# A two-layer decoder trunk in split fp32r: seven raw weight buffers for four, eight Strassen blocks for seven, and the next layer's transposes one block forward

## The chip, the core and the metric

The kernel runs on one core of one Trainium2 chip. The time is that of one execution on the device, in microseconds; lower is better. Three runs of the kernel before are shown, and their median stands for it. Beside them one execution was profiled: its trace gives for every instruction the engine, the start, the duration and what it waited for. Engines are written as the profile writes them: PE is TensorE's matmul, PEld its weight load, DVE is VectorE, ACT is ScalarE, SP is SyncE, whose queue issues the loads.

## The reference

Two layers are applied to 256 tokens of 1024 features, in fp32. Each layer has a mixing part (three branches from one wide input projection, merged by gates) and an MLP with a squared ReLU; each part is normalised before and after and added to h.

```python
# per layer; T = 256, D_MODEL = 1024, D_FF = 4096
u = rms_norm(h, norm_mix_pre)
z = u @ w_in                      # q | k | v | rnn_x | rnn_y | pool | gates
mix = gated_merge(z, attention(q, k, v) @ w_attn_br,
                  gelu(rnn_y) * rg_lru(conv4(rnn_x)) @ w_rnn_br,
                  multi_scale_pool(pool) @ w_pool_br) @ w_out
h = h + rms_norm(mix, norm_mix_post)
m = rms_norm(h, norm_mlp_pre)
hid = relu(m @ w_mlp_up) ** 2     # 256 x 4096
h = h + rms_norm(hid @ w_mlp_down, norm_mlp_post)
```

## The kernel before

**Products in three passes.** Every fp32 operand is split into a part hi in the type fp32r and a remainder lo (`split`: ACT copies the source into hi, L90; DVE subtracts it from the source, L91). A product is the sum of hi x hi, hi x lo and lo x hi, three matmuls into one PSUM bank (`mm3`, L98 to L100; `by_pass`, L309, does the same in three sweeps).

**Weights.** All weights of both layers are packed as 316 units of 128 x 1024 fp32, 512 KB each, in the order of use. `load_to` takes a buffer of the pool `raws` and issues the load on SP's queue (L140). `split_to(n)` splits units up to n into the pools `his` and `los` (eight buffers each: names wh and wl), and then calls `load_to(n + 3)`, so that the loads run three units ahead with the four raw buffers. A raw buffer is free again when both ACT's copy and DVE's subtraction have read it; SP's queue works in order, and a load whose buffer isn't free holds up what stands behind it. PSUM has eight banks, handed out in turn from one pool; tmp has 28 buffers of 2 KB per partition, acts three of each kind.

**The MLP.** The hidden width is cut into 16 blocks of 256. An up unit (`up`, through `w_unit`) makes one block's hidden values for all tokens: 48 matmuls of 256 columns, then Relu (L735) and Square on ACT, which leave z. The down product of a block is a 256 x 256 by 256 x 1024 matrix product. For the first `nstr = NBLK - PLAIN` blocks it is done by Strassen's seven products in Winograd's form (`down`): seven products of 128 x 128 by 128 x 512, accumulated over the blocks in seven PSUM banks (pr), 21 matmuls of 512 columns a block in place of 24. They need sums: `weight_sums` adds halves of two raw units on DVE (wsum, L763, L767, L768) and splits the first (dh, dl) and a half of the second (bh, bl); `weight_forms` splits the two sums (sh, sl, one name for both); `hidden_forms` makes four differences of the hidden values on DVE (sm, L746 to L749) and splits them and z itself into xf, in two pieces of 384 and 512 columns. `drain` combines the seven banks. The remaining `PLAIN` blocks are plain (`hidden_split`, `plain`: 24 matmuls); the last `LAST = 3` of them run together, one quarter of the output after the other (tokens tt, columns nh).

**How the two are interleaved.** `UPS` says how many up units stand in each Strassen block: one up unit, four products, another up unit, three products; or, with one, the up unit and then all seven products. The first up unit of a block is also the place at which the sums and hidden forms of the next block are issued. While the Strassen part runs, seven PSUM banks hold products and the eighth (ps) takes the up units in turn, so that an up unit's first matmul waits for the Relu of the one before it. `up_first` makes the first two blocks' hidden values another way: in rows by tokens, with wh as the moving operand (ps <- mh), followed by transposes. In it, `mlp_in(1)` makes the second half of the MLP's input: transposes of h on PE (L222, `to_features`), copies to mh on ACT (L228), remainders ml on DVE (L230).

**The seam between layers.** After the first 128 tokens' last plain block, `residual(0)` (square sums on ACT, yg on DVE L270, h L275) and `mix_norm(0)` (un, L321) run while the other 128 tokens' plain blocks go on; `mix_features(0)` then transposes un (L222) and makes uh (ACT L228) and ul (DVE L230), and `residual(1)`, `mix_norm(1)` follow at the end. The next layer's first matmuls (ps <- wh,uh, L309) read uh and ul.

**What sets the order.** The program is written in the order above, but a scheduler orders the instructions of each engine by priority: the place in the program, and 200 places earlier for what is wrapped in `hp` (residual, mix_norm, mix_features and the MLP's to_features). An instruction on one engine's list waits for its operands in its turn, with all behind it. Which buffers and which waits arise follows from these lists and from the pools' sizes. GpSimd does nearly nothing; all transfers are issued by SP, but for two small ones by ACT.

Of the kernel before, what the change touches and what calls it, by code (L numbers as in the profile page):

```python
# [16 lines left out]
L = 2  # L17
# [6 lines left out]
HU_COLS = 1024  # L24
HP = 200
WARM = 12
NRAW = 4
NTMP = 28
NHI = 8
MID = 1  # L30
# [3 lines left out]
RGD = 4  # L34
FINE = (8, 8)

PLAIN = 9
LAST = 3

UPS = (2, 2, 2, 2, 2, 2, 1)  # L40
NBLK = 16
SQRT_2_PI = 0.7978845608028654

# [15 lines left out]
def trunk(ctx, tc, x, wts, rgw, par, gpost, eye, ctab, out):  # L59
    nc = tc.nc  # L60
    V, A, PE, G = nc.vector, nc.scalar, nc.tensor, nc.gpsimd

    const = ctx.enter_context(tc.tile_pool(name="const", bufs=1))
    raws = ctx.enter_context(tc.tile_pool(name="raws", bufs=NRAW))
    his = ctx.enter_context(tc.tile_pool(name="his", bufs=NHI))
# [13 lines left out]
    def ttile(shape, dt=F32, nm="t"):  # L79
        return tmp.tile(shape, dt, tag="t", name=nm)  # L80
# [7 lines left out]
    def split(hi, lo, src, scale=None):  # L88
        if scale is None:
            A.activation(hi, src, AF.Copy)  # L90
            V.tensor_tensor(out=lo, in0=src, in1=hi.bitcast(F32), op=ALU.subtract)  # L91
        else:
            A.activation(hi, src, AF.Copy, scale=scale)
            V.scalar_tensor_tensor(out=lo, in0=src, scalar=scale, in1=hi.bitcast(F32),
                                   op0=ALU.mult, op1=ALU.subtract)
# [34 lines left out]
    st = {"load": 0, "split": 0, "use": 0}  # L130
# [5 lines left out]
    def load_to(n):  # L136
        while st["load"] < min(n, NHU):
            i = st["load"]
            r = raws.tile([P, HU_COLS], F32, tag="raw", name=f"raw{i}")
            nc.sync.dma_start(r[:], wts[i])  # L140
            raw_t[i] = r
            st["load"] += 1

    def split_to(n):
        while st["split"] < min(n, NHU):
            i = st["split"]
            load_to(i + 1)
            r = raw_t.pop(i)
            wh = his.tile([P, HU_COLS], F32R, tag="wh", name=f"wh{i}")
            wl = los.tile([P, HU_COLS], F32R, tag="wl", name=f"wl{i}")  # L150
            parts = 2 if i in fine else 1
            for k in range(parts):
                sl = slice(k * HU_COLS // parts, (k + 1) * HU_COLS // parts)
                split(wh[:, sl], wl[:, sl], r[:, sl])
            hu_t[i] = (wh, wl)
            st["split"] += 1
        load_to(n + 3)

    def take(n):
        split_to(st["use"] + n)  # L160
        r = [hu_t.pop(st["use"] + i) for i in range(n)]
        st["use"] += n
        return r

    def ahead():
        split_to(st["use"] + AHEAD)
# [91 lines left out]
    @hp  # L258
    def residual(tt, banks, scale, gB):

        yg = []
        ss = stile(2)
        for nh in range(2):
            square_sum(banks[nh][:], ss[:, nh:nh + 1], scale)
            t = ttile([P, 512], nm="yg")
            gs = gB[:, nh * 512:(nh + 1) * 512]
            if isinstance(scale, float):
                V.tensor_tensor(out=t[:], in0=banks[nh][:], in1=gs, op=ALU.mult)
            else:
                V.scalar_tensor_tensor(out=t[:], in0=banks[nh][:], scalar=scale, in1=gs, op0=ALU.mult, op1=ALU.mult)  # L270
            yg.append(t)
        rs = rsqrt(total(ss))
        for nh in range(2):
            sl = slice(nh * 512, (nh + 1) * 512)
            V.scalar_tensor_tensor(out=h[:, tt, sl], in0=yg[nh][:], scalar=rs, in1=h[:, tt, sl],  # L275
                                   op0=ALU.mult, op1=ALU.add)
# [38 lines left out]
    @hp  # L315
    def mix_norm(tt):
        rstd = rsqrt(sumsq(halves(tt)))
        u = []
        for x_ in halves(tt):
            t = ttile([P, 512], nm="un")  # L320
            V.tensor_scalar(t[:], x_, rstd, None, op0=ALU.mult)  # L321
            u.append(t)
        return u

    @hp
    def mix_features(tt, u, l):
        to_features(tt, u, prm[:, l, PG_PRE:PG_PRE + 8], uh, ul)
# [3 lines left out]
    nc.sync.dma_start(h[:, 1, :], x[P:T, :])  # L331
    un = [mix_norm(0)]
    split_to(1)
    to_features(0, un[0], prm[:, 0, PG_PRE:PG_PRE + 8], uh, ul, between=lambda: split_to(2))
    split_to(3)
# [4 lines left out]
    for l in range(L):  # L340
# [357 lines left out]
        nc.sync.dma_start(gB[:], gpost[l, 1])  # L698
        nstr = NBLK - PLAIN
        prods = {}  # L700
# [30 lines left out]
        def up(j):  # L731
            ps = w_unit(take(2), uh, ul)
            tick()
            z = ttile([P, 2, T], nm="z")
            A.activation(z[:], ps[:], AF.Relu)  # L735
            A.activation(z[:], z[:], AF.Square)
            zs[j] = z
# [18 lines left out]
        def weight_sums(j):  # L756

            load_to(st["split"] + 2)
            r0, r1 = raw_t.pop(st["split"]), raw_t.pop(st["split"] + 1)
            st["split"] += 2  # L760
            st["use"] += 2
            t8 = acts.tile([P, 4, 512], F32, tag="lo", name="wsum")
            V.tensor_tensor(out=t8[:, 0:2, :], in0=r0.rearrange("p (b n) -> p b n", b=2),  # L763
                            in1=r1[:, 0:512].unsqueeze(1).to_broadcast([P, 2, 512]), op=ALU.add)
            w1 = (his.tile([P, HU_COLS], F32R, tag="wh", name="dh"), los.tile([P, HU_COLS], F32R, tag="wl", name="dl"))
            w4 = (ttile([P, 512], F32R, nm="bh"), ttile([P, 512], F32R, nm="bl"))
            V.tensor_tensor(out=t8[:, 2, :], in0=t8[:, 0, :], in1=r0[:, 512:1024], op=ALU.add)  # L767
            V.tensor_tensor(out=t8[:, 3, :], in0=t8[:, 2, :], in1=r1[:, 512:1024], op=ALU.add)  # L768
            split(w1[0][:], w1[1][:], r0[:])
            split(w4[0][:], w4[1][:], r1[:, 512:1024])  # L770
            wforms[j] = [w1, w4, t8]
            load_to(st["split"] + 3)

        def weight_forms(j):
            t8 = wforms[j].pop()
# [5 lines left out]
        def down(j, part):  # L781
            f = forms[j]
            w1, w4, w2, w3 = wforms[j]
            lo_, up_ = slice(0, 512), slice(512, 1024)

            for p, blk, w, cs in ((1, 2, w1, up_), (3, 6, w1, lo_), (2, 0, w4, lo_), (7, 5, w2, lo_), (5, 3, w2, up_),
                                  (6, 4, w3, lo_), (4, 1, w3, up_))[part]:
                if p not in prods:
                    prods[p] = bank([P, 512], nm="pr")
                first, last = j == 0, j == nstr - 1 and p in (1, 5, 6, 7)  # L790
                mm3(prods[p][:], f[:, 0, blk, :], f[:, 1, blk, :], w[0][:, cs], w[1][:, cs], first, last)
# [9 lines left out]
        for j in range(nstr):  # L801
            for i in range(UPS[j]):
                up(nup)
# [4 lines left out]
                if nup < NBLK:  # L808
                    split_to(st["use"] + 2)
                down(j, slice(0, 7) if UPS[j] == 1 else (slice(0, 4), slice(4, 7))[i])  # L810
            del forms[j], wforms[j]
# [20 lines left out]
        def plain(j, hus, tt, nh):  # L832
            for k in range(2):
                wh, wl = hus[k]
                cs, tsl = slice(nh * 512, (nh + 1) * 512), slice(tt * P, (tt + 1) * P)
                mm3(tgt[tt][nh][:], hids[j][:, 0, k, tsl], hids[j][:, 1, k, tsl], wh[:, cs], wl[:, cs],
                    tt == 1 and nh == 1 and j == nstr and k == 0, j == NBLK - 1 and k == 1)
# [22 lines left out]
        for tt in range(2):  # L860
            for nh in range(2):
                for b in range(LAST):
                    if tt == 1 and nh == 1 and b == LAST - 1 and l + 1 < L:
                        mix_features(0, un[0], l + 1)
                    plain(NBLK - LAST + b, hus[2 * b:2 * b + 2], tt, nh)
            ys = [rest[tt][nh] for nh in range(2)]
            for nh in range(2):
                V.tensor_tensor(out=ys[nh][:], in0=tgt[tt][nh][:], in1=ys[nh][:], op=ALU.add)
            residual(tt, ys, msq[tt], gB)
            if l + 1 < L:  # L870
                un.append(mix_norm(tt))
            else:
                for hf in range(2):
                    sl = slice(hf * 512, (hf + 1) * 512)
                    nc.sync.dma_start(out[tt * P:(tt + 1) * P, sl], h[:, tt, sl])
# [37 lines left out]
def _layout(i):  # L913
    qc = np.concatenate([np.arange(hd * 64, hd * 64 + 64) for hd in _HEADS])
    units, rg, par, gp = [], [], [], []
    for l in range(L):
# [18 lines left out]
        dn = i["w_mlp_down"][l].reshape(NBLK, 2, P, D)  # L935
        nstr = NBLK - PLAIN
        pairs = [np.stack([np.concatenate([d[c][:, 512:], d[1 - c][:, :512]], 1) for c in range(2)]) for d in dn]
        units += [up[0], up[1], up[2], pairs[0], up[3]]
        nup = 3
        for j in range(nstr):  # L940
            for n in range(UPS[j]):
                nup += 1
# [28 lines left out]

# [10 lines left out]
```

## Time and profile before

| | |
|---|---|
| median of 3 runs | 961.85 us (959.25 to 962.14) |
| the profiled execution's own time | 960.85 us |
| its span in the trace | 959.1 us |
| granted TensorE clock | 0.996 |
| DMA, mean over the span | 181 GB/s, 173.29 MB in all |
| L91 on DVE (subtractions for lo) | x316, 349.8 us, mean 1126 ns |
| L90 on ACT (copies to hi) | x316, 302.2 us, mean 987 ns |
| loads of raw units, median from issue to landing | 4.3 us |

How to read the rows that follow: a group of instructions reads line, engine, operation, output <- inputs, partitions x elements; a row that begins with a time gives the start within the span and the duration in us, and in brackets the wait just before it and what ended it. A matmul's duration reaches into the next one's, so that a TensorE row's duration isn't what it costs; the distance of the starts is. In a row of a stretch of time, the figures behind its bounds are length, then busy time (and instructions) of PE, PEld, DVE, ACT, POOL and SP, the granted clock, the busy share of the 16 DMA engines and their GB/s. A row of the waits gives the wait's sum, its count and its longest.

### The profile page before, as it was taken

Reading aid. Unit: us, or ns where it says so; the run is one execution under the profiler, and the core shown is the slowest. Engines: PE = TensorE matmul, PEld = TensorE weight load, DVE = VectorE, ACT = ScalarE, POOL = GpSimd, SP = SyncE. Lnnn points to the kernel's source line nnn. Section 1 sums busy time; section 2 is a strip of 40 time slices with the busy share of each in tenths; the row PEclk is TensorE's granted clock in tenths of the full one; section 3 lists DMA queues with packets and bytes.
Section 4 is the critical chain, followed back from the end, with each engine's and each line's share of the span. In section 5 each row is a group of like instructions: output and inputs, shape, how many; then the busy total and the mean of one; then the engine's idle time right before and its main releaser. Section 6 shows DMA issues by size and latency. Waiting matters only on the chain.

```text
span 959.1 us, 15057 instructions
## 1 busy us (share of the span) xinstructions
PE 946.3 (99%) x5674; PEld 827.5 (86%) x5674; DVE 730.0 (76%) x1253; ACT 620.5 (65%) x1049; POOL 2.6 (0%) x20
## 2 busy tenths in 40 slices
PE   8999999999999999999999999999999999999997
PEld 5898988988888998998878989788888899999885
DVE  6878786779768987867586769777897599787753
ACT  7754864788736766675376657556895467666741
POOL 0000000000000000000000000000000000000000
PEclk9999999999999999999999999999999999999999
DMA  7766456453754556566457536536358265646641
GB/s 269 250 201 194 132 158 205 149 192 111 243 174 154 208 170 209 168 216 217 132 178 255 171 123 194 186 114 221 123 174 262 90 210 186 223 169 207 197 151 44
DMA packets 48745, 173.29 MB, mean 181 GB/s; under 512 B 5408, under 2 KB 5792, under 8 KB 48672
## 3 DMA queue, kind: packets, MB, share of 16 engines
q1 hardware_dynamic: 48384, 172.16, 54.7%
q8 instruction: 44, 0.72, 0.3%
q14 instruction: 29, 0.24, 0.1%
q10 hardware_dynamic: 288, 0.17, 0.1%
HBM read 171.26 MB, written 1.05 MB: 180 GB/s over the span
## 4 chain that ended last, share of the span: by engine, by line
PE 88%; DMA 5%; DVE 4%; ACT 1%; issue 1%; DVEq 0%; SPq 0%; ACTq 0%
PE ps L98 20%; PE ps L100 20%; PE ps L99 20%; PE ps L309 7%; DMA raw<-wts 5%; PE pr L100 5%; PE pr L99 5%; PE pr L98 5%; PE ps L397 1%; PE ps L445 1%; DVE wl L91 1%; PE ps L434 1%; ACT wh L90 1%; PE ps L222 0%; PE ps L377 0%
## 5 line engine op out<-in xcount | busy, mean ns | idle before, releaser
L91 DVE TENSOR_TENSOR wl<-raw,wh 128x1024 fp32r<-128x1024 f32 (+1 forms) x316 | 349.8, 1126 | 121.4 <-ACT wh L90 113.8
L90 ACT ACTIVATE wh<-raw 128x1024 fp32r<-128x1024 f32 (+1 forms) x316 | 302.2, 987 | 192.7 <-PE ps L100 60.2
L98 PE MATMUL ps<-mh,wh 128*128 128x256 f32 x448 | 127.2, 284 | 1.3 <-ACT z L735 1.3
L100 PE MATMUL ps<-mh,wl 128*128 128x256 f32 x448 | 126.8, 283 | 0.0
L99 PE MATMUL ps<-ml,wh 128*128 128x256 f32 x448 | 126.7, 283 | 0.0
L98 PE MATMUL ps<-uh,wh 128*128 128x256 f32 x384 | 109.0, 284 | 0.0
L99 PE MATMUL ps<-ul,wh 128*128 128x256 f32 x384 | 108.6, 283 | 0.0
L100 PE MATMUL ps<-uh,wl 128*128 128x256 f32 x384 | 108.6, 283 | 0.0
L98 PEld LDWEIGHTS ps<-mh,wh 128*128 128x128 f32 x448 | 85.9, 192 | 3.7 <-ACT z L735 2.8
L99 PEld LDWEIGHTS ps<-ml,wh 128*128 128x128 f32 x448 | 85.9, 192 | 0.7
L100 PEld LDWEIGHTS ps<-mh,wl 128*128 128x128 f32 x448 | 85.9, 192 | 0.0
L98 PE MATMUL ps<-wh,uh 128*128 128x512 f32 x200 | 79.8, 399 | 1.0 <-ACT uh L228 1.0
L100 PE MATMUL ps<-wh,ul 128*128 128x512 f32 x200 | 78.6, 393 | 0.1
L99 PE MATMUL ps<-wl,uh 128*128 128x512 f32 x200 | 78.5, 393 | 0.0
L98 PEld LDWEIGHTS ps<-uh,wh 128*128 128x128 f32 x384 | 73.6, 192 | 1.1 <-issue 0.7
L99 PEld LDWEIGHTS ps<-ul,wh 128*128 128x128 f32 x384 | 73.6, 192 | 0.4
L100 PEld LDWEIGHTS ps<-uh,wl 128*128 128x128 f32 x384 | 73.6, 192 | 0.0
L98 PE MATMUL pr<-wh,hid 128*128 128x512 f32 x144 | 56.1, 390 | 0.0
L100 PE MATMUL pr<-wh,hid 128*128 128x512 f32 x144 | 56.0, 389 | 0.0
L99 PE MATMUL pr<-wl,hid 128*128 128x512 f32 x144 | 56.0, 389 | 0.0
L98 PEld LDWEIGHTS ps<-wh,uh 128*128 128x128 f32 x200 | 37.9, 189 | 11.1 <-issue 2.3
L100 PEld LDWEIGHTS ps<-wh,ul 128*128 128x128 f32 x200 | 37.9, 189 | 8.9 <-DVE ul L230 0.8
(234 smaller groups left out, 1916.5 us busy)
## 6 DMA issues: line engine op xcount, KB each, us to landing
raw<-wts SPq DMA_DIRECT2D x316, 512.0 KB, 4.3
gB<-gpost SPq DMA_DIRECT2D x4, 512.0 KB, 5.4
rg<-rgw SPq DMA_DIRECT2D x8, 256.0 KB, 3.8
out<-h SPq DMA_DIRECT2D x4, 256.0 KB, 2.0
h<-x SPq DMA_DIRECT2D x2, 256.0 KB, 3.6
h<-x SPq DMA_DIRECT2D x1, 512.0 KB, 7.5
cst<-ctab SPq DMA_DIRECT2D x1, 168.0 KB, 3.7
prm<-par ACTq DMA_DIRECT2D x1, 104.0 KB, 4.0
```

The lines of the kernel that those rows point to most:

```text
L90: A.activation(hi, src, AF.Copy)
L91: V.tensor_tensor(out=lo, in0=src, in1=hi.bitcast(F32), op=ALU.subtract)
L98: PE.matmul(o, lh, rh, start=start, stop=False, **kw)
L99: PE.matmul(o, lh, rl, start=False, stop=False, **kw)
L100: PE.matmul(o, ll, rh, start=False, stop=stop, **kw)
L309: PE.matmul(o, xx[:, c, tsl], ww[c], start=(n == 0 and c == 0), stop=(n == 2 and c == 7))
L397: PE.matmul(sc[hd // hp][:, hd % hp, :], qT[a, j // 2][rows, j % 2, blk * P:(blk + 1) * P], kTs[0][rows, a, 0:w], start=True, stop=True)
L434: PE.transpose(ps[:, g, :], g8["p"](4 * b + g)[:, kt * P:(kt + 1) * P], ident)
L445: PE.matmul(ps[b * 64:b * 64 + 64, :, :], vt[kt][:, 256 + kv * 64:256 + kv * 64 + 64], g8[b, kt][:], start=(kt == 0), stop=(kt == nk - 1))
```

## The change

The edit has four parts.

- The pool `raws` has seven buffers instead of four, and the two calls that load ahead reach six units ahead instead of three (in `weight_sums`, five units past the pair just taken instead of three). The kernel is built with a smaller area in SBUF for DMA descriptors (`dynamic_dma_scratch_size=1024` bytes per partition, where the default was 16384).
- `PLAIN` is 8 instead of 9: eight blocks of 16 go by Strassen's seven products.
- `UPS` spreads the 13 up units over eight Strassen blocks as 2, 2, 2, 1, 2, 1, 2, 1 instead of 2, 2, 2, 2, 2, 2, 1 over seven. `_layout` packs the units in that order.
- `mix_features(0)` of the next layer is called ahead of the last plain block but one of the last quarter, instead of ahead of the last.

```diff
-NRAW = 4
+NRAW = 7
...
-PLAIN = 9
+PLAIN = 8
 LAST = 3

-UPS = (2, 2, 2, 2, 2, 2, 1)
+UPS = (2, 2, 2, 1, 2, 1, 2, 1)
...
             st["split"] += 1
-        load_to(n + 3)
+        load_to(n + NRAW - 1)
...
             wforms[j] = [w1, w4, t8]
-            load_to(st["split"] + 3)
+            load_to(st["split"] + NRAW - 2)
...
                 for b in range(LAST):
-                    if tt == 1 and nh == 1 and b == LAST - 1 and l + 1 < L:
+                    if tt == 1 and nh == 1 and b == LAST - 2 and l + 1 < L:
                         mix_features(0, un[0], l + 1)
...
-    nc = bacc.Bacc("TRN2", target_bir_lowering=False, num_devices=1)
+    nc = bacc.Bacc("TRN2", target_bir_lowering=False, num_devices=1, dynamic_dma_scratch_size=1024)
```

What it moves is seen in each engine's list. On SP three more raw loads of the first layer stand ahead of the constants table (cst, L337), and the first gain row (gB, L668) stands at place 28 of the list instead of 11; the number of loads is the same. On PE there are 5668 matmuls instead of 5674: 48 fewer of pr <- hid (432 to 384) and 42 more of pr <- xf (294 to 336).

**The MLP's start, on PE.** The place is `up_first` of the first layer: by_pass over the first 128 tokens, with the transposes of h (operand idt, the identity) for the other 128 put in. Before:

```order
L309 MATMUL ps<-wh_3201,mh 128x256 x4
L309 MATMUL ps<-wh_3207,mh 128x256 x4
L309 MATMUL ps<-wh_3201,ml 128x256 x3
L222 MATMUL ps<-idt,h 128x128 x4
L309 MATMUL ps<-wh_3201,ml 128x256
L222 MATMUL ps<-idt,h 128x128 x4
L309 MATMUL ps<-wh_3207,ml 128x256 x4
L309 MATMUL ps<-wl_3202,mh 128x256 x4
```

And after the change, where the numbers of the names are others but 3207, 3213 and 3208 stand for the same weights as 3201, 3207 and 3202 above:

```order
L309 MATMUL ps<-wh_3207,mh 128x256 x4
L309 MATMUL ps<-wh_3213,mh 128x256 x4
L309 MATMUL ps<-wh_3207,ml 128x256 x4
L309 MATMUL ps<-wh_3213,ml 128x256 x4
L222 MATMUL ps<-idt,h 128x128 x4
L309 MATMUL ps<-wl_3208,mh 128x256
L222 MATMUL ps<-idt,h 128x128 x4
L309 MATMUL ps<-wl_3208,mh 128x256 x3
```

Five more matmuls stand ahead of the transposes of h.

**The same place, on DVE.** h is finished at L275; then come the first weight sum (L763), the remainders ml of the second 128 tokens (L230) and the square of the first hidden values (zt, L726). Before:

```order
L275 SCALAR_TENSOR_TENSOR h<-yg,s,h 128x512 x2
L91 TENSOR_TENSOR wl_3356<-raw_3213,wh_3355 128x512
L763 TENSOR_TENSOR wsum<-raw_3215,raw_3361 128x1024
L230 SCALAR_TENSOR_TENSOR ml<-ps,prm,mh 128x128 x8
L726 TENSOR_TENSOR zt<-zt 128x512
L767 TENSOR_TENSOR wsum<-wsum,raw_3215 128x512
L91 TENSOR_TENSOR dl<-raw_3215,dh 128x1024
```

And after:

```order
L275 SCALAR_TENSOR_TENSOR h<-yg,s,h 128x512 x2
L763 TENSOR_TENSOR wsum<-raw_3201,raw_3203 128x1024
L91 TENSOR_TENSOR dl<-raw_3201,dh 128x1024
L230 SCALAR_TENSOR_TENSOR ml<-ps,prm,mh 128x128 x8
L726 TENSOR_TENSOR zt<-zt 128x512
L767 TENSOR_TENSOR wsum<-wsum,raw_3201 128x512
L91 TENSOR_TENSOR wl_3452<-raw_3219,wh_3451 128x1024
```

The remainder dl of the first block's weights stands ahead of the eight ml pieces instead of behind them, and one half of a wl that stood behind h has gone ahead of it.

**A Strassen block, on DVE.** The place is the fourth block of the first layer, which has two up units before and one after. Ahead of the rows shown, both lists have the next block's first sum (wsum, L763), dl, a wl, the first piece of xf and a second wl. Before:

```order
L91 TENSOR_TENSOR wl126_4208<-raw126_4119,wh126_4207 128x1024
L91 TENSOR_TENSOR wl127_4212<-raw127_4139,wh127_4211 128x1024
L91 TENSOR_TENSOR bl_4110<-raw123_4032,bh_4109 128x512
L746 TENSOR_TENSOR sm_4121<-z_3642 128x128
L747 TENSOR_TENSOR sm_4121<-z_3642 128x128
L748 TENSOR_TENSOR sm_4121<-sm_4121,z_3642 128x128
L749 TENSOR_TENSOR sm_4121<-z_3642,sm_4121 128x128
L91 TENSOR_TENSOR sl_4229<-wsum_4105,sh_4228 128x1024
L91 TENSOR_TENSOR xf_4126<-sm_4121,xf_4126 128x512
L763 TENSOR_TENSOR wsum_4288<-raw128_4141,raw129_4215 128x1024
```

And after, in the block with one up unit:

```order
L767 TENSOR_TENSOR wsum_4230<-wsum_4230,raw126_4038 128x512
L768 TENSOR_TENSOR wsum_4230<-wsum_4230,raw127_4040 128x512
L91 TENSOR_TENSOR sl_4171<-wsum_4111,sh_4170 128x1024
L91 TENSOR_TENSOR sl_4175<-wsum_4111,sh_4174 128x1024
L91 TENSOR_TENSOR bl_4116<-raw123_3960,bh_4115 128x512
L746 TENSOR_TENSOR sm_4125<-z_3648 128x128
L747 TENSOR_TENSOR sm_4125<-z_3648 128x128
L748 TENSOR_TENSOR sm_4125<-sm_4125,z_3648 128x128
L749 TENSOR_TENSOR sm_4125<-z_3648,sm_4125 128x128
L91 TENSOR_TENSOR dl_4233<-raw126_4038,dh_4232 128x1024
L91 TENSOR_TENSOR wl128_4255<-raw128_4123,wh128_4254 128x1024
L91 TENSOR_TENSOR xf_4130<-sm_4125,xf_4130 128x512
```

The two wl of the second up unit (126 and 127) are gone, since those units are now the block's weights; both sl, a dl of the block after and one wl stand between the list's start and the last piece of xf.

**The seam between layers, on DVE.** The place is the end of the first layer's MLP: un of the first 128 tokens is made at L321, then the other 128 tokens' residual (us, yg). Before:

```order
L321 TENSOR_SCALAR un<-h,s 128x512 x2
L91 TENSOR_TENSOR wl_5154<-raw_5141,wh_5153 128x512
L270 SCALAR_TENSOR_TENSOR yg<-us,s,gB_3199 128x512
L91 TENSOR_TENSOR wl_5154<-raw_5141,wh_5153 128x512
L868 TENSOR_TENSOR us<-pr,us 128x512
L230 SCALAR_TENSOR_TENSOR ul<-ps,prm,uh 128x128
L270 SCALAR_TENSOR_TENSOR yg<-us,s,gB_3199 128x512
L230 SCALAR_TENSOR_TENSOR ul<-ps,prm,uh 128x128
```

And after:

```order
L321 TENSOR_SCALAR un<-h,s 128x512 x2
L91 TENSOR_TENSOR wl_5176<-raw_4977,wh_5175 128x512
L270 SCALAR_TENSOR_TENSOR yg<-us,s,gB_3205 128x512
L91 TENSOR_TENSOR wl_5176<-raw_4977,wh_5175 128x512
L868 TENSOR_TENSOR us<-pr,us 128x512
L230 SCALAR_TENSOR_TENSOR ul<-ps,prm,uh 128x128 x4
L270 SCALAR_TENSOR_TENSOR yg<-us,s,gB_3205 128x512
```

Four pieces of ul stand ahead of the last yg, where one stood. On PE the transposes of the first 128 tokens' un keep their place, three plain matmuls before the end of the quarter, and those of the other 128 tokens stand seven matmuls later.

## The prediction

> **What bounds the kernel now.** I read the page's busy times and chain first, then TensorE's instructions in order of time, then the waits inside the MLP.
>
> ```profile
> span 959.1 us, 15057 instructions
> PE 946.3 (99%) x5674; PEld 827.5 (86%) x5674; DVE 730.0 (76%) x1253; ACT 620.5 (65%) x1049; POOL 2.6 (0%) x20
> PE 88%; DMA 5%; DVE 4%; ACT 1%; issue 1%; DVEq 0%; SPq 0%; ACTq 0%
> q1 hardware_dynamic: 48384, 172.16, 54.7%
> ```
>
> TensorE is busy nearly always, but a matmul's shown duration overlaps the next one's, so I go by starts. These two rows are the first and last of 45 plain-block matmuls, each of 512 columns:
>
> ```profile
> 469.82 0.39 PE L98 MATMUL pr<-wh,hid 128*128 128x512 f32 x1
> ...
> 479.80 0.39 PE L100 MATMUL pr<-wh,hid 128*128 128x512 f32 x1
> ```
>
> (479.80 - 469.82) / 44 = 0.227 us from start to start. By this rate, stalls outside the start and end of the program lie almost all in and around the MLP, where the Strassen blocks run. Time can come from fewer matmuls or from those stalls; all that DVE, ACT or DMA do elsewhere is hidden.
>
> **The change, part by part.**
>
> *(a) One Strassen block more, one plain block less, per layer.* A plain block has 2 x 2 x 2 x 3 = 24 matmuls of 512 columns, a Strassen block 7 x 3 = 21. Two layers: 6 matmuls fewer, 6 x 0.227 = 1.36 us, all on the path. [...]
>
> The block costs more on the helpers. One Strassen block with two up units is 16.34 us long:
>
> ```profile
> 396.95:413.29 16.34, 16.34 (x118) 15.30 (x118) 13.15 (x18) 10.60 (x15) 0.00 (x0) 1.00 0.61 196
> ...
> 304.36 1.12 PE L309 MATMUL ps<-wh,mh 128*128 128x256 f32 x8
> 305.32 0.52 PE L309 MATMUL ps<-wh,ml 128*128 128x256 f32 x3
> ```
>
> DVE is busy 13.15 us of it, ACT 10.60. The 256-column matmuls start every 0.96/8 = 0.12 us, so an up unit (48 of them) is 5.76 us. Without one up unit a block is 16.34 - 5.76 = 10.58 us of TensorE, and DVE loses two splits of about 1.14 us: 13.15 - 2.28 = 10.87 us. A one-unit block therefore asks 0.3 us more of DVE than it lasts; a two-unit block leaves 3.2 us. The list has such blocks fourth, sixth and eighth (the last prepares no successor), each behind a two-unit block, so the overdraft of 0.3 us is covered by DVE's lead. How much lead? With raw data present, DVE finishes the third block's last form about when the fourth block's up unit starts (T). I then follow the order shown ahead: wsum, dl, wl, xf, wl, two wsum halves (to T+6), two sl behind ACT's copies, which wait for the up unit to free two buffers (T+8.3), bl, four differences, dl, wl, and the last xf at about T+12.5. TensorE needs that xf six matmuls into the next block, at T + 10.58 + 5.76 + 5 x 0.23 = T+17.4. About 5 us are spare; I take 0. From above: were DVE's 3.2 us of idle time per block not recoverable, two one-unit blocks per layer would each be 3.5 us late, 14 us in all.
>
> *(b) Seven raw buffers.* Here is what they can remove:
>
> ```profile
> ACT wh L90 <- DMA raw<-wts: 20.3, 12, 3.0
> PE ps L98 <- ACT z L735: 1.0, 1, 1.0
> ...
> 357.52 4.96 DMA raw<-wts
> 362.58 1.06 ACT wh L90
> 363.64 0.49 ACT z L735
> ...
> 362.81 0.39 PE L100 MATMUL pr<-sh,xf 128*128 128x512 f32 x1
> 364.18 0.39 PE L98 MATMUL ps<-mh,wh 128*128 128x256 f32 x1 [0.98 <-ACT z L735]
> ...
> 834.77 0.39 PE L100 MATMUL pr<-sh,xf 128*128 128x512 f32 x1
> 835.46 0.39 PE L98 MATMUL ps<-mh,wh 128*128 128x256 f32 x1 [0.30 <-ACT z L735]
> ```
>
> The first two rows are waits from 300 to 440 us, the next three the chain. During Strassen seven PSUM banks hold products and one holds the up unit's result, so the next up unit waits for its Relu (z). ACT works in order: the copy ahead of the Relu waits 4.96 us for a DMA whose buffer came free late. Loss: 364.18 - 362.81 - 0.23 = 1.14 us, and 0.46 in layer 1. With three more buffers the DMA was issued long before: I take 1.60 (ends 0 and 1.60).
>
> At the MLP's start:
>
> ```profile
> 306.32 0.63 PE L222 MATMUL ps<-idt,h 128*128 128x128 f32 x4 [0.49 <-issue]
> ...
> 776.60 0.52 PE L309 MATMUL ps<-wh,ml 128*128 128x256 f32 x3
> 777.25 0.63 PE L222 MATMUL ps<-idt,h 128*128 128x128 f32 x4
> ...
> 779.74 1.12 PE L309 MATMUL ps<-wh,mh 128*128 128x256 f32 x8
> 781.22 1.42 PE L309 MATMUL ps<-wh,ml 128*128 128x256 f32 x5 [0.35 <-DVE ml L230]
> 782.47 0.28 PE L98 MATMUL ps<-mh,wh 128*128 128x256 f32 x1
> ...
> 779.67 1.23 DVE L763 TENSOR_TENSOR wsum<-raw,raw 128x1024 f32<-128x1024 f32 x1 [1.31 <-DMA raw<-wts]
> ```
>
> The transposes of h start 306.32 - (305.32 + 0.36) = 0.64 us late in layer 0, 0.29 in layer 1. In the new order five more matmuls (0.60 us) stand ahead of them and fill this. In layer 1 the ml matmuls lose 781.22 - 780.70 = 0.52 and 1.25 - 0.60 = 0.65: DVE made wsum first, and that waited 1.31 us for raw data. The data will be there; but a dl of 1.14 us now stands between wsum and ml, so some waiting may stay. Of 2.10 I take 1.60 (ends 0 and 2.10).
>
> The first Strassen block's wait for its hidden forms:
>
> ```profile
> 328.16 0.40 PE L98 MATMUL pr<-bh,xf 128*128 128x512 f32 x1
> 328.90 0.50 PE L100 MATMUL pr<-dh,xf 128*128 128x512 f32 x1 [0.34 <-DVE xf L91]
> ...
> 800.21 0.40 PE L98 MATMUL pr<-bh,xf 128*128 128x512 f32 x1
> 800.85 0.50 PE L100 MATMUL pr<-dh,xf 128*128 128x512 f32 x1 [0.24 <-DVE xf L91]
> ```
>
> 0.51 + 0.41 = 0.92 us. Those forms come from the hidden transposes, not from DMA, and DVE has a queue behind them; I take 0.4 (ends 0 and 0.92).
>
> Past its buffers the change moves DMA issues: three more raw loads go ahead of the constants table, and the gain rows (gB) move by a few loads.
>
> ```profile
> h<-x SPq DMA_DIRECT2D x1, 512.0 KB, 7.5
> ...
> 0.00:25.00 25.00, 21.95 (x83) 14.40 (x84) 16.80 (x50) 18.35 (x46) 0.33 (x5) 0.93 0.79 267
> ...
> 22.09 0.23 DVE L350 TENSOR_TENSOR rt<-qkv,cst 128x64 f32<-128x64 f32 x1 [0.66 <-ACT qkv L367]
> ...
> 39.99 1.31 PE ps L377 x12
> ```
>
> 267 GB/s at a share of 0.79 is 338 GB/s at full share. The table then lands behind seven raws, 3.67 MB or 10.9 us after x's second half (about 10.1 us): near 21 us, with its first reader at 22.09 and TensorE's need of the result at 39.99. Cost 0; at worst DVE is 1 us late under 18 us of cover. The first raws keep their place ahead in the queue. Elsewhere ACT's waits for raw data cost nothing now, so removing them gains nothing.
>
> *(c) The smaller descriptor area.* All issues stand on SP's and ACT's queues and GpSimd's has no row, so 0 us; were hardware queues to use the area, every load would be late (a rival). [...]
>
> *(d) The transposes.* In the built order un's first transposes do not move: three plain matmuls still follow them. What moves is DVE: four of the eight ul pieces go ahead of the next residual step, and un's second transposes stand seven matmuls later.
>
> ```profile
> 481.69 2.07 PE L309 MATMUL ps<-wh,uh 128*128 128x512 f32 x8
> ...
> 487.55 1.99 PE L309 MATMUL ps<-wl,uh 128*128 128x512 f32 x8
> ...
> 486.30 0.86 DVE L230 SCALAR_TENSOR_TENSOR ul<-ps,prm,uh 128x128 fp32r<-128x128 f32 x3
> ```
>
> The 21 matmuls between the first two rows need 21 x 0.227 = 4.77 us and took 5.86: 1.09 lost, the last ul coming at 486.30. ul comes sooner, the second half's norm some 0.6 us later, under 1.6 us of added matmuls. I take 0.5 (ends -0.5 and 1.09).
>
> **Sum.** 1.36 + 1.60 + 1.60 + 0.4 + 0.5 = 5.46 us. The profiled execution took 960.85 us around its span of 959.1, so 955.4; the median shown, 961.85, lies 1.0 above it, so 956.4 us.
>
> **Rivals.** *Only the matmuls count:* new waits fill the holes. ACT still runs another split before most Relus:
>
> ```profile
> 419.20 1.06 ACT L90 ACTIVATE wh<-raw 128x1024 fp32r<-128x1024 f32 x1 [0.38 <-PE ps L99]
> 420.17 0.57 ACT L735 ACTIVATE z<-ps 128x512 f32<-128x512 f32 x1
> ...
> 421.19 0.28 PE L98 MATMUL ps<-mh,wh 128*128 128x256 f32 x1
> ```
>
> Then 961.85 - 1.36 = 960.5. Chance 0.19.
>
> *DVE becomes the bound in one-unit blocks:* 0.3 us overdrawn plus the 3.2 us it idles per block today. With 14 us lost and 5.5 gained, 970; it ends above today's time once each of the four blocks is more than 5.46/4 = 1.4 us late, that is, once the 5 us of lead are gone. Chance 0.06.
>
> *The single free PSUM bank:* above, the Relu ends at 420.74 and the next up unit starts at 421.19, 0.45 us of margin. The added block keeps that regime longer. If each of 13 units per layer were 0.3 us late, 7.8 us go: 956.4 + 7.8 = 964. The trace's only two losses had a DMA behind them. Chance 0.03. [...]
>
> *The descriptor area throttles the hardware queues:* at 54.7% DMA share a third less rate would reach 82% and starve bursts: over 970. Chance 0.02.
>
> *All listed stalls go:* 1.36 + 1.60 + 2.10 + 0.92 + 1.09 = 7.07, so 954.8; chance 0.10, the forecast 0.60.
>
> **How the numbers follow.** The runs shown spread over 2.9 us, so 0.3% (2.9 us) is about what this measurement can tell from no change. Forecast and "all stalls go" are faster by more: 0.70. "Only the matmuls" is the same: 0.19. The other three are slower: 0.11. The range runs from all stalls gone less the runs' spread of some 1.8 us, 953.0, to 961.5 (matmuls alone plus 1 us of spread); 2 in 10 at most lie outside.
>
> **What would show it.** 5668 PE instructions; pr matmuls on hid 384, on xf 336. No 0.3 us wait of L98 for z; ACT's waits for raw in the MLP well under 20 us; L222 without a wait near 306 and 777; one-unit blocks about 10.6 us long. It is wrong if one-unit blocks last over 11 us, if L98 waits for z or DVE's wl in each, or if raw loads land later than 4.3 us after issue and TensorE waits on them.

## The result, and the profile after

The changed kernel takes 952.73 us (median of 6 runs, 952.53 to 954.02); the kernel before, run beside it, 960.84 us (6 runs, 959.25 to 962.14). The ratio is 0.9919, 95% interval 0.9906 to 0.9932: faster by 8.1 us, where 5.46 had been forecast. The time lies 0.3 us under the range given; taken as a ratio of the 961.85 us that stood with the prediction it would be 954.1, inside it.

The page of the changed kernel, its first lines and the engines' shares of the chain that ended last:

```profile
span 951.0 us, 15062 instructions
PE 941.2 (99%) x5668; PEld 826.1 (87%) x5668; DVE 738.7 (78%) x1273; ACT 623.9 (66%) x1055; POOL 2.5 (0%) x20
...
PE 98%; ACT 1%; DMA 1%; DVE 0%; issue 0%; SPq 0%; DVEq 0%
```

The chain was 88% PE, 5% DMA and 4% DVE; it is 98% PE now. In the waits from 300 to 440 us (engine, line, what it waits for, then sum, count and longest) ACT no longer waits for a load; its largest wait is for TensorE, and the only waits for a load there cost DVE 1.0 us:

```profile
ACT wh L90 <- PE ps L99: 12.1, 12, 2.6
...
DVE wsum L763 <- DMA raw<-wts: 1.0, 2, 0.7
```

To see where the 8.1 us of span went, I cut both traces at the starts of the same instructions: the first QK product (L397) of each layer, the first transposes of h before the MLP, the first Strassen product, the first plain one. The two cuts around the first layer's Strassen part are these rows, of before and then of after:

```profile
327.01 0.40 PE L98 MATMUL pr<-dh,xf 128*128 128x512 f32 x1
...
431.74 0.39 PE L98 MATMUL pr<-wh,hid 128*128 128x512 f32 x1
```

```profile
325.48 0.40 PE L98 MATMUL pr<-dh,xf 128*128 128x512 f32 x1
...
433.06 0.39 PE L98 MATMUL pr<-wh,hid 128*128 128x512 f32 x1
```

431.74 - 327.01 = 104.73 us for seven blocks, 433.06 - 325.48 = 107.58 for eight. An eighth block's 21 matmuls are 4.77 us at 0.227, so stalls of 1.92 us went in this layer. The stages that changed:

| stage | before, us | after, us | counted matmuls | stalls, us |
|---|---|---|---|---|
| opening, to the first L397 | 58.82 | 57.75 | 0 | -1.07 |
| MLP's start, layers 0 and 1 | 32.60, 33.39 | 32.12, 32.14 | 0 | -0.48, -1.25 |
| Strassen part, layers 0 and 1 | 104.73, 104.03 | 107.58, 107.57 | +4.77 each | -1.92, -1.23 |
| plain blocks and the seam to layer 1 | 98.30 | 92.04 | -5.45 | -0.81 |
| plain blocks of layer 1 | 48.73 | 43.29 | -5.45 | 0 |

Matmuls: 2 x 4.77 - 2 x 5.45 = -1.36 us. Stalls: -6.76. Together -8.12; the parts not listed, mixing and the end, differ by less than 0.1 us.

### The profile page after: what moved, and what is told of

It is laid out like the page before. It is cut to its first block, busy times and chain, and to the rows that moved or that the text cites. A ratio compares the mean times of both kernels' runs of the same rounds, so it can differ in the third digit from the quotient of the medians.

```text
span 951.0 us, 15062 instructions
## 1 busy us (share of the span) xinstructions
PE 941.2 (99%) x5668; PEld 826.1 (87%) x5668; DVE 738.7 (78%) x1273; ACT 623.9 (66%) x1055; POOL 2.5 (0%) x20
## 4 chain that ended last, share of the span: by engine, by line
PE 98%; ACT 1%; DMA 1%; DVE 0%; issue 0%; SPq 0%; DVEq 0%
PE ps L98 22%; PE ps L100 22%; PE ps L99 22%; PE ps L309 9%; PE pr L98 6%; PE pr L99 6%; PE pr L100 6%; PE ps L397 1%; PE ps L445 1%; PE ps L434 1%; PE ps L222 1%; DMA raw<-wts 1%; PE ps L377 0%; PE ps L625 0%; ACT junk L235 0%; ACT uh L228 0%
## 5 line engine op out<-in xcount | busy, mean ns | idle before, releaser
L91 DVE TENSOR_TENSOR wl<-raw,wh 128x1024 fp32r<-128x1024 f32 (+1 forms) x312 | 344.5, 1123 | 87.1 <-ACT wh L90 78.3
L90 ACT ACTIVATE wh<-raw 128x1024 fp32r<-128x1024 f32 (+1 forms) x312 | 296.3, 986 | 160.3 <-PE ps L100 60.9
L98 PE MATMUL pr<-wh,hid 128*128 128x512 f32 x128 | 49.9, 390 | 0.0
L100 PE MATMUL pr<-wh,hid 128*128 128x512 f32 x128 | 49.8, 389 | 0.0
L99 PE MATMUL pr<-wl,hid 128*128 128x512 f32 x128 | 49.8, 389 | 0.0
L90 ACT ACTIVATE sh<-wsum 128x1024 fp32r<-128x1024 f32 x32 | 33.8, 1057 | 24.2 <-PE ps L99 21.3
L91 DVE TENSOR_TENSOR sl<-wsum,sh 128x1024 fp32r<-128x1024 f32 x32 | 38.9, 1221 | 12.7 <-ACT sh L90 12.2
```

The costliest lines, as they stand in the source:

```text
L98: PE.matmul(o, lh, rh, start=start, stop=False, **kw)
L99: PE.matmul(o, lh, rl, start=False, stop=False, **kw)
L100: PE.matmul(o, ll, rh, start=False, stop=stop, **kw)
```

## The experiments

Every kernel was timed beside the kernel before on the same chip; ratios are against that. Before's median was 960.0 to 961.6 us in these comparisons (7 to 17 runs each, single runs from 958.0 to 965.1), while each kernel with seven raw buffers spread over 0.4 to 2.6 us (4 to 6 runs).

### The parts one at a time

**The seven buffers alone** (old blocks, old seam):

```diff
-NRAW = 4
+NRAW = 7
...
-        load_to(n + 3)
+        load_to(n + NRAW - 1)
...
-            load_to(st["split"] + 3)
+            load_to(st["split"] + NRAW - 2)
...
-    nc = bacc.Bacc("TRN2", target_bir_lowering=False, num_devices=1)
+    nc = bacc.Bacc("TRN2", target_bir_lowering=False, num_devices=1, dynamic_dma_scratch_size=1024)
```

> Before with the seven raw buffers alone (loads six ahead, descriptor area 1024), still seven Strassen blocks and the old place of the transposes. Theory: the loads were late, so that all the stalls of TensorE in and around the Strassen part go without a new block: 3.2 us inside it (the after trace lost none there) and 1.7 us at the MLP's start; 960.8 - 4.9 = 955.9 us. If the first 40 us also gain by it (the after trace was 1.0 us ahead there), 954.9. Rival, that the stalls went because of the new order of the blocks: 960.8, no gain.

Measured: 955.71 us (5 runs, 955.54 to 955.98), ratio 0.9942 (0.9930 to 0.9954). Its Strassen part in the first layer, cut as above:

```profile
326.19 0.40 PE L98 MATMUL pr<-dh,xf 128*128 128x512 f32 x1
...
429.03 0.39 PE L98 MATMUL pr<-wh,hid 128*128 128x512 f32 x1
```

102.84 us, in layer 1 102.86; with a block of 4.77 more that is after's 107.6. The MLP's starts last 32.18 and 32.14, as after. So all the stalls that the profile of before has in these two stages belong to the buffers, with the order of the lists that comes with them: here too the five more matmuls stand ahead of the transposes of h. The seam lasts 98.30 us, as before; the opening, 58.41, has a section below.

**Eight blocks alone** (four buffers, old seam):

```diff
-PLAIN = 9
+PLAIN = 8
...
-UPS = (2, 2, 2, 2, 2, 2, 1)
+UPS = (2, 2, 2, 1, 2, 1, 2, 1)
```

> Before with eight Strassen blocks and the new spread of up units alone, four raw buffers. Theory: 6 matmuls of 0.227 us fewer, -1.4 us, with the old stalls left where they were: 959.5. Rival: blocks with one up unit need raw units that four buffers can't bring in time (four units in 10.6 us), so TensorE waits for a Relu or a wl in each of four blocks, 1 us or more: 962 or above.

Measured: 965.98 us (6 runs, 963.44 to 967.92), ratio 1.0046 (1.0028 to 1.0063). The theory's 959.5 was wrong, the rival right: six matmuls fewer, and 4.5 us slower. The Strassen parts last 114.21 and 111.75 us, 6.6 and 4.2 more than after's. Its waits from 300 to 440 us, the up units that came late, and the chain that leads to the last of them:

```profile
ACT wh L90 <- DMA raw<-wts: 22.5, 13, 4.5
...
DVE wsum L763 <- DMA raw<-wts: 9.7, 4, 3.3
...
PE ps L98 <- ACT z L735: 5.0, 3, 2.7
```

```profile
365.12 0.38 PE L98 MATMUL ps<-mh,wh 128*128 128x256 f32 x1 [2.21 <-ACT z L735]
...
392.44 0.39 PE L98 MATMUL ps<-mh,wh 128*128 128x256 f32 x1 [0.16 <-ACT z L735]
...
422.38 0.39 PE L98 MATMUL ps<-mh,wh 128*128 128x256 f32 x1 [2.67 <-ACT z L735]
```

```profile
416.03 1.15 DVE dl L91
...
417.19 3.51 DMA raw<-wts
...
420.78 1.06 ACT wh L90
421.84 0.49 ACT z L735
...
422.38 0.39 PE ps L98
```

The chain tells the mechanism. DVE's subtraction dl is the last reader of a raw unit; the next load starts when it ends (416.03 + 1.15 = 417.18, load from 417.19) and takes 3.51 us. ACT's copy of the new unit stands ahead of the Relu (z), the Relu holds the one free PSUM bank, and TensorE's up unit starts 2.67 us late. Here the parts don't add: buffers alone save 5.6 us, blocks alone cost 4.5, both together (next run, without the seam) save 6.9.

**After without the moved transposes:**

```diff
-                    if tt == 1 and nh == 1 and b == LAST - 2 and l + 1 < L:
+                    if tt == 1 and nh == 1 and b == LAST - 1 and l + 1 < L:
```

> After without the moved transposes. Theory: the seam between the layers loses again what it lost before (1.1 us of waits for ul, of which after keeps 0.3): 952.7 + 0.8 = 953.5. Rival, that the seam's gain came from the raw buffers: 952.7.

Measured: 954.05 us (6 runs, 953.37 to 955.94), ratio 0.9928 (0.9916 to 0.9941). The 21 matmuls of the seam that were counted in the prediction, here and then after:

```profile
477.29 2.06 PE L309 MATMUL ps<-wh,uh 128*128 128x512 f32 x8
...
483.13 2.00 PE L309 MATMUL ps<-wl,uh 128*128 128x512 f32 x8
```

```profile
477.58 2.05 PE L309 MATMUL ps<-wh,uh 128*128 128x512 f32 x8
...
482.66 2.00 PE L309 MATMUL ps<-wl,uh 128*128 128x512 f32 x8
```

5.84 us, of which 1.07 are lost, against 5.08 and 0.31. The whole stage is 92.85 against 92.04. The seam's 0.8 us is the work of the moved transposes alone; the two times, whose intervals overlap, would not show it.

**The descriptor area alone:**

```diff
-    nc = bacc.Bacc("TRN2", target_bir_lowering=False, num_devices=1)
+    nc = bacc.Bacc("TRN2", target_bir_lowering=False, num_devices=1, dynamic_dma_scratch_size=1024)
```

> Before with the smaller descriptor area alone; all transfers are issued by SP and ACT. Theory: no effect, 960.8 within the runs' spread of 1.5 us. Rival: the area changes how soon the first loads land (in the after trace the first x landed 0.4 us and the first raw unit 0.8 us sooner): 959.8 with a first 40 us that are 1.0 us shorter. Rival the other way, that the hardware queues use the area: above 965.

Measured: 961.92 us (12 runs, 959.11 to 963.25), ratio 1.0002 (0.9991 to 1.0014). No effect, with every load issued by SP or ACT; what uses the area, no run shows. Its trace shows the old blocks on four buffers a second time: Strassen parts of 105.38 and 105.60 us, 5.3 us of stalls over raws_only's where the profile of before had 3.1, but MLP's starts of 32.17 and 32.43 us, only 0.3 us of stalls where before had 1.7.

### How many buffers, and how far ahead

**Five buffers in after:**

```diff
-NRAW = 7
+NRAW = 5
```

> After with five raw buffers in place of seven (loads four ahead). Theory: what costs with four is that a load is issued only when DVE's last reader lets go of a buffer, 4 to 6 us before ACT needs the data; a fifth buffer brings each load about one unit (2.7 us) sooner, which covers most of the late ones: the Strassen part of each layer lasts 107.6 us as with seven, or at most 1 us more, 953 to 955 in all. Rival, that seven are needed because a pair of units is held through a whole block: the Strassen part stays 2 us or more longer in each layer, 957 or above.

Measured: 955.40 us (7 runs, 954.18 to 956.33), ratio 0.9942 (0.9922 to 0.9962), a little above the theory's 953 to 955. The Strassen parts are 107.58 and 107.57 us, those of seven buffers: one buffer more took away all of the 10.8 us that four lost there in the profile of blocks_only. (The profiled execution, 954.18 us, is the fastest of the seven; what the others lost beyond it was not traced.) What five still lose is at the MLP's start, 33.18 and 32.93 us for 32.1:

```profile
305.58 1.06 ACT L90 ACTIVATE wh<-raw 128x1024 fp32r<-128x1024 f32 x1 [2.70 <-DMA raw<-wts]
306.55 2.16 ACT L228 ACTIVATE mh<-ps,prm 128x128 fp32r<-128x128 f32 x8
```

```profile
306.94 1.93 PE L309 MATMUL ps<-wh,mh 128*128 128x256 f32 x7 [0.18 <-ACT mh L228]
```

ACT waits 2.70 us for a load, with the copies mh behind it, and then TensorE's matmuls follow at the pace of those copies.

**Seven buffers, loads asked for three ahead:**

```diff
-        load_to(n + NRAW - 1)
+        load_to(n + 3)
...
-            load_to(st["split"] + NRAW - 2)
+            load_to(st["split"] + 3)
```

> After with the seven buffers, but the calls ask for loads only three units ahead again, as before. Theory: a load waits for a free buffer alone, and SP's list of loads keeps its order, so that the distance in the program does nothing: 952.7, with the Strassen parts 107.6 us long. Rival, that the greater distance was half of the gain: 955 or above.

Measured: 953.15 us (4 runs, 952.70 to 953.65), ratio 0.9920 (0.9896 to 0.9944); Strassen parts 107.58 and 107.57, MLP's starts 32.17 and 32.15. The distance does nothing, which fits a queue that runs down its list until a buffer is missing (in the profile of before SP's loads waited 258 times for a wl on DVE, the reader of a raw buffer, 620.4 us in all): the number of buffers alone says how far that is.

### Is DVE the limit of blocks with one up unit?

**The three one-unit blocks in a row:**

```diff
-UPS = (2, 2, 2, 1, 2, 1, 2, 1)
+UPS = (2, 2, 2, 2, 1, 1, 1, 2)
```

> After with the three blocks of one up unit in a row (2, 2, 2, 2, 1, 1, 1, 2). Theory: 3 x 0.3 us is overdrawn out of a lead of some 5 us on DVE, so nothing is lost: 952.7 with Strassen parts of 107.6 us. Rival, that a block of two units is needed behind each to recover: the second and third block of one unit each lose 1 us or more, 956.7 or above.

Measured: 953.58 us (4 runs, 952.77 to 954.23), ratio 0.9924 (0.9900 to 0.9949); Strassen parts 107.61 and 107.56. Nothing is lost.

**Nine blocks:**

```diff
-PLAIN = 8
+PLAIN = 7
...
-UPS = (2, 2, 2, 1, 2, 1, 2, 1)
+UPS = (2, 2, 1, 2, 1, 2, 1, 1, 1)
```

> After with nine Strassen blocks (up units 2, 2, 1, 2, 1, 2, 1, 1, 1). Theory: 6 matmuls of 0.227 us fewer again and DVE's lead carries five blocks of one unit, 0.3 us overdrawn each: 952.7 - 1.4 = 951.4. Rival, DVE as the bound: in the three blocks with one unit at the end the lead is gone, TensorE waits for xf or sl, 1 us or more a block in each layer: 955 or above.

Measured: 952.16 us (6 runs, 951.23 to 952.45), ratio 0.9908 (0.9888 to 0.9927). Its opening was 58.34 us in the profile; without the openings the spans are 950.3 - 58.34 = 891.96 and 951.0 - 57.75 = 893.25, 1.29 apart for the 1.36 expected.

**Twelve blocks:**

```diff
-PLAIN = 8
+PLAIN = 4
...
-UPS = (2, 2, 2, 1, 2, 1, 2, 1)
+UPS = (2, 1, 1, 1, 1, 1, 1, 1, 1, 1, 1, 1)
```

> After with twelve Strassen blocks of 16, all but the first with one up unit. Theory: DVE's instructions start 1.14 us apart where it works without a pause (a 128x1024 subtraction is shown as 1.22), so that a block of one unit asks 10.5 of its 10.6 us and nothing is overdrawn; 24 matmuls of 0.227 us fewer than after, 952.7 - 5.4 = 947.3. Rival: with no slack on DVE its waits for ACT's copies (up to 2.6 us each in after) can't be made up, and each block beyond the first few is 0.5 us or more late, ten blocks in two layers: 957 or above.

Measured: 947.51 us (4 runs, 947.29 to 948.57), ratio 0.9873 (0.9856 to 0.9890). The Strassen parts are 126.68 and 126.70 us, which is 107.58 + 4 x 4.77 = 126.66. Some six one-unit blocks, by busy time of each engine (PE, PEld, DVE, ACT, POOL), with the clock, the DMA share and GB/s:

```profile
353.00:417.00 64.00, 64.00 (x419) 58.69 (x418) 63.76 (x91) 47.13 (x62) 0.00 (x0) 1.00 0.62 205
```

DVE is busy 63.76 of 64.00 us and TensorE isn't held up once (busy 64.00 of 64.00 us). With one bank for the up units in every block, no up unit lost anything, so here the single bank costs nothing as long as the Relu isn't queued behind a late load, as it was in blocks_only, where an up unit started 2.67 us late.

**Thirteen blocks**, first with the last two plain blocks grouped instead of three (edits to the twelve):

```diff
-PLAIN = 4
-LAST = 3
+PLAIN = 3
+LAST = 2
...
-UPS = (2, 1, 1, 1, 1, 1, 1, 1, 1, 1, 1, 1)
+UPS = (1,) * 13
```

> Twelve blocks taken one further: thirteen Strassen blocks of one up unit each, and the last two plain blocks grouped instead of three. Theory: 6 matmuls of 0.227 us fewer than with twelve, 947.5 - 1.4 = 946.1, with each Strassen block 10.55 us long. Rival: DVE was busy 63.76 of 64.00 us in the one-unit blocks of twelve, and the first block now gives it no second up unit's time to get ahead; xf or sl come late, or with two grouped blocks the seam's residual and transposes lose their cover: a wait of 1 us or more in each layer, 948 or above.

Measured: 949.98 us (4 runs, 949.56 to 950.46), ratio 0.9882 (0.9857 to 0.9906): no gain over twelve, where 1.4 us were expected. The Strassen parts are 131.45 us, 126.68 + 4.77: they lost nothing. The seam did:

```profile
473.74 0.39 PE L100 MATMUL pr<-wh,hid 128*128 128x512 f32 x1
476.02 1.12 PE L222 MATMUL ps<-idt,un 128*128 128x128 f32 x8 [1.89 <-DVE un L321]
477.46 0.79 PE L309 MATMUL ps<-wh,uh 128*128 128x512 f32 x1 [0.33 <-ACT uh L228]
```

```profile
477.00:480.20 3.20, 2.88 (x9) 2.16 (x8) 3.20 (x9) 3.20 (x13) 0.00 (x0) 0.50 0.41 138
```

TensorE waits for the residual and the norm, and after that pause its granted clock is 0.50 for 3.2 us.

**Thirteen with three grouped** (against the run above; no plain block is left outside the group, so drain is called ahead of it):

```diff
-LAST = 2
+LAST = 3
...
+        if nstr == NBLK - LAST:
+            tgt[1][1] = bank([P, 512], nm="pr")
+            rest = drain()
         for j in range(NBLK - LAST, NBLK):
```

> Thirteen Strassen blocks again, but the last three blocks grouped as in after (no plain block of its own is left; drain is called ahead of the group). Theory: what thirteen lost with two grouped blocks was the cover of the seam alone (TensorE waited 1.89 us for un and 0.33 for uh and then ran 3 us at a granted clock of 0.50); with six more matmuls a quarter as cover the Strassen parts stay at 131.45 us and the seam has no wait: 947.5 - 1.4 = 946.1. Rival: without a plain block before the group the split of the hidden values and drain come late, and the seam or the group's start waits 1 us or more: 947.5 or above.

Measured: 946.13 us (5 runs, 946.01 to 946.61), ratio 0.9841 (0.9823 to 0.9860). The same place has no wait:

```profile
472.56 1.09 PE L222 MATMUL ps<-idt,un 128*128 128x128 f32 x8
473.41 0.48 PE L98 MATMUL pr<-wh,hid 128*128 128x512 f32 x1
473.73 0.39 PE L99 MATMUL pr<-wl,hid 128*128 128x512 f32 x1
```

The stage of plain blocks and seam is 64.72 us instead of 68.39 with the same 72 matmuls. This is the fastest version of the study, 6.6 us below the changed kernel's median.

### The opening

The first 58 us gained 1.07 us in the two profiles. Before and then after: ACT's copies of the first raw unit, the copies uh behind them, which the first product needs, and the clock some us later (behind it DMA share and GB/s):

```profile
7.61 1.15 ACT L90 ACTIVATE wh<-raw 128x512 fp32r<-128x512 f32 x2 [1.37 <-DMA raw<-wts]
8.67 1.12 ACT L228 ACTIVATE uh<-ps,prm 128x128 fp32r<-128x128 f32 x4
...
9.60:12.60 3.00, 2.91 (x8) 1.91 (x7) 2.48 (x7) 3.00 (x10) 0.00 (x0) 0.50 0.94 352
```

```profile
6.78 1.15 ACT L90 ACTIVATE wh<-raw 128x512 fp32r<-128x512 f32 x2 [0.91 <-DMA raw<-wts]
7.84 1.12 ACT L228 ACTIVATE uh<-ps,prm 128x128 fp32r<-128x128 f32 x4
...
9.00:12.00 3.00, 2.60 (x10) 1.72 (x10) 2.48 (x7) 3.00 (x10) 0.00 (x0) 1.00 1.01 414
```

The first raw unit landed 0.83 us sooner, uh came as much sooner, and the clock did not fall. Over the runs the opening goes with the time at which that copy starts: 59.64 us for 8.28 (area_only), 58.34 for 7.35 (nine_blocks), 57.26 for 6.04 (five_raws). The load is issued at 1.64 or 1.65 us in every profile, so the number of buffers can't move it. The three profiles with four buffers do have long openings (58.45 to 59.64, the eleven others 57.26 to 58.72), but from the start of that copy to the first QK product all fourteen take 50.9 to 51.4 us, with four buffers as with more. So I take the 1.07 us for the run's, not the change's.

**Fillers in the opening of after:**

```diff
+FILL = 6
...
     to_features(0, un[0], prm[:, 0, PG_PRE:PG_PRE + 8], uh, ul, between=lambda: split_to(2))
+    for i in range(FILL):
+        PE.matmul(wps[:], warm[:, 0:P], warm[:], start=True, stop=True)
     split_to(3)
```

> After with six more 512-column matmuls on the constant tile warm, written behind the first transposes of un (two of them end up ahead of these, four behind). Theory: the opening (up to the first L397) lasts 57.3 to 59.6 us from run to run, by when the first weights land and whether the granted clock falls to 0.5 after TensorE has been idle for about 1 us at 8 us; the four matmuls fill that hole, the clock stays at 1.00 and the opening lasts at most 57.9 us: 952.4 with a spread under 0.6. Rival, that the opening is set by x and the weights alone and the fillers only stand in the way: 58.5 us or more, 953.5.

Measured: 953.84 us (5 runs, 953.71 to 954.10), ratio 0.9936 (0.9923 to 0.9948). The clock was 1.00 from 6 to 15 us in the profile, but the opening lasted 58.72 us: the rival's number. The copy of the first raw unit starts only at 7.73 us there, and from it to the first QK product it is 50.99 us, as without fillers: a late load made that opening long, and the fillers neither shortened it nor stood in the way. Why all five runs took 953.7 to 954.1 us stays open.

## Why the prediction was right or wrong

**The sign and most of the mechanism held.** Late loads behind four buffers were most of the stalls, and seven removed them.

| step of the prediction | forecast, us | measured, us | shown by |
|---|---|---|---|
| (a) six matmuls fewer | 1.36 | 1.36 | the stages; nine and twelve blocks |
| (b) Relu (z) and first hidden forms (xf) | 1.60 + 0.4 | 3.15 | seven buffers alone: 3.07 |
| (b) MLP's start | 1.60 | 1.73 | seven buffers alone: 1.67 |
| (c) descriptor area | 0 | 0 | area alone |
| (d) transposes | 0.5 | 0.81 | after without them |
| opening | not in the sum | 1.07 | varies by run |

**The step that was wrong is the price of the first Strassen block's forms, 0.4 of 0.92 us,** taken low because they "come from the hidden transposes, not from DMA". That follows what xf is made from; it leaves out what stands ahead of it in the lists. Before, and then after:

```profile
325.93 1.06 ACT L90 ACTIVATE wh<-raw 128x1024 fp32r<-128x1024 f32 x1 [0.66 <-DMA raw<-wts]
...
327.02 1.23 DVE L91 TENSOR_TENSOR wl<-raw,wh 128x1024 fp32r<-128x1024 f32 x1 [0.48 <-ACT wh L90]
328.16 0.69 DVE L91 TENSOR_TENSOR xf<-sm,xf 128x512 fp32r<-128x512 f32 x1
```

```profile
324.53 1.22 DVE L91 TENSOR_TENSOR wl<-raw,wh 128x1024 fp32r<-128x1024 f32 x1
325.67 0.68 DVE L91 TENSOR_TENSOR xf<-sm,xf 128x512 fp32r<-128x512 f32 x1
```

In before ACT's copy of a raw unit waited 0.66 us for its load, DVE's wl waited 0.48 us for that copy, and the last piece of xf stood behind wl: it ended at 328.85, and the matmul that needs it started at 328.90. In layer 1 it is the same (0.78 us for the load, 0.59 for the copy). With the data there, wl and xf follow without a pause, so the whole 0.92 went. Each of the four waits in the Strassen parts also cost some 0.1 us in the matmul behind it: 0.34 us from start to start instead of 0.227 between the prediction's row at 328.90, the late matmul, and this one:

```profile
329.24 0.39 PE L99 MATMUL pr<-bl,xf 128*128 128x512 f32 x1
```

1.60 + 0.92 + 0.4 = 2.9 of the 3.15 us. Of the 2.66 us by which the stages' 8.12 exceed the forecast 5.46, the Strassen parts are 1.15, the seam 0.31, the MLP's start 0.13 and the opening, which the sum does not have, 1.07. "All listed stalls go", the rival given 0.10, is what happened, and the time came out 2.1 us below its 954.8: 1.07 is the opening, and 1.0 the base, since the median of three runs (961.85) lay that much above the profiled execution and the median of six (960.84) does not.

**A second error is older than the sum:** it took one profile's stalls for the kernel's. With four buffers 3.1 us were lost over the Strassen parts in one trace, 5.3 in another of the same program but for the descriptor area; at the MLP's start it was 1.7 and 0.3. That the forecast for each place came so near is in part luck: it was priced on the very profile against which it is checked.

**The rivals.** *Only the matmuls count* fell with the seven buffers alone. *DVE becomes the bound* fell: the estimate of 10.87 us of DVE work in a one-unit block started from a busy time, 13.15 us, in which an instruction before a pause counts in full, 1.22 us for a subtraction whose successor, where there is no pause, starts 1.14 us later. In after the fourth block lasted what TensorE needs, 10.58 us:

```profile
374.47:385.05 10.58, 10.58 (x71) 9.70 (x70) 9.62 (x14) 7.54 (x10) 0.00 (x0) 1.00 0.70 225
```

By starts the two-unit block asks 12.8 us and the one-unit block 12.8 - 2.28 = 10.5, and twelve and thirteen blocks ran without a loss and without a lead to spend. *The single free PSUM bank* cost nothing with enough buffers and 5.0 us from 300 to 440 us with eight blocks on four. *The descriptor area* did nothing (area_only, ratio 1.0002); no run shows what uses the area, so that the forecast's 0 was the author's estimate, which the time bore out. What no rival said is that (a) alone would be slower: its gain was priced with buffers it doesn't have by itself. One-unit blocks use hardly more raw units for their length (4 in 10.58 us, 6 in 16.33), so the rate isn't the cause; the time for which a buffer is taken can be. From the issue of its load to the end of its last reader, the first layer of blocks_only keeps the first raw unit of a weight pair for 13.0 to 14.0 us (until dl) and the second for 18.4 to 20.8 (until bl), together 31 at least, and a raw unit of an up unit for 5.9 or more. My estimate from these: a one-unit block needs 31 + 2 x 5.9 = 43 us of buffer time or more, and four buffers give it 4 x 10.58 = 42.3, five 52.9; a two-unit block needs 55 or more of its 65.3. That fits the loss with four and none with five; no run varies the holding time alone.

## What to carry to other kernels

When an engine that works in order waits for a load, follow what stands behind it in its list, through every engine, before pricing the wait: the Relu, the last piece of xf and, in the opening, uh each stood behind a late copy or its remainder. Here the number of buffers, not the distance at which loads are asked for (953.15 us at three ahead, 952.73 at six), set how early a load starts, and a fifth buffer took most of the gain (955.4 us, where seven gave 952.7). Price a part of a change that leans on another part with and without it, and measure how full an engine is by the distance of its starts, not by its busy time alone.

## What the runs showed that was not expected

- With four buffers the kernel's time spread over 7 us (958.0 to 965.1); with seven, over 2.6 us or less, in fewer runs each. The two traces of the old blocks on four buffers differ by 2.2 us in the Strassen parts, by 1.4 us the other way at the MLP's start and by 0.8 us in the opening: where a late load costs time changes from run to run.
- A pause of TensorE of 1.89 us and 0.33 us behind it went with 3.2 us at a granted clock of 0.50 (thirteen blocks with two grouped); before's opening shows 3 us of it as well. From the last matmul ahead of the pause to the slow stretch 3.0 us passed (473.97 to 477.00), and 2.8 us in the opening (6.26 to 9.07), in both with eight transposes in between. Whether the pauses bring the lower clock, no run shows: in before's opening TensorE waited 0.76 and 0.96 us around those transposes, in that of raws_only 1.06 and 0.82 us, and there the clock stayed at 1.00. In all, pause and slow stretch, that seam lost 68.39 - 64.72 = 3.67 us.
- Eight Strassen blocks made the kernel 4.5 us slower with four raw buffers, and in the profiled run with five no block lost anything: there was no middle.
